# Summing four of a pair's seven products in one PSUM bank, with ScalarE copies between the groups

## The chip, the cores and the metric

One core of one Trainium2 chip runs the whole program. The metric is the device time of one execution in microseconds (us). TensorE (PE) multiplies matrices into PSUM, an accumulator memory of eight banks; VectorE (DVE) and ScalarE (ACT) read PSUM and work in SBUF; GpSimd (POOL) and SyncE (SP) mostly issue DMAs here. Each engine works through its own queue in order and waits on semaphores of the others.

## The reference

Two layers of a decoder trunk over 544 token columns (512 of a prompt, 32 of eight short samples). What matters is the large matrix products: two SwiGLU feed-forward blocks of each layer, and the input projection of the mixers with its sigmoid gates.

```
h = rmsnorm(x, g);  gate, up = split(h @ w_up)          # 1024 -> 2 x 2816
x = x + 0.5 * (silu(gate) * up) @ w_down                # 2816 -> 1024, twice in a layer
z = rmsnorm(x, g_mix) @ w_in                            # 1024 -> 6144
u = gelu(z[u]);  g = sigmoid(z[gates])                  # the parts of z that the change touches
merged = g0 * y_a + g1 * y_b + g2 * y_c;  x = x + merged @ w_o
```

## The kernel before

**Tiling.** Activations lie transposed in SBUF: 128 partitions by 544 tokens, and `HT` = 272 is half of them. Every product is made of three matmuls, since operands are split into a high and a low part: low weight by high input, high by high, high by low. Weights stream from memory as *units* of 512 columns. `unit` first stages later units: it issues loads (SP, for some units with an accumulating POOL DMA, L223 to L231), adds two raw blocks on VectorE (L237, `split_add`), takes the high part on ScalarE (L244, `split_hi`) and the low part on VectorE (L249, `split_lo`), four to six units ahead of the one in use. The order on every engine is the order in which the code is written; a tile framework adds the semaphores.

**Pairs.** Two blocks of 128 outputs by 544 tokens make a *pair*. `s_pair` computes it with seven products of half size in place of eight, in Winograd's form: the weights and the token halves are summed and subtracted beforehand (`s_inputs`, `split_add`), seven products named W21, R3, W22, R1, R2, R4 and W12 are made (`PRODUCTS`), and their results are combined into the four quarters of the pair. Each product is 12 matmuls of 128x272 (`mm_s`, L325), one unit of weights. A pair's halves are called h1 and h2; its two result tiles are `a` (s1) and `b` (s2). One ScalarE copy (L579) and seven VectorE operations (L581, L583, L587, L588, L589, L591, L593) read the products from PSUM. There are 109 pairs. 81 are in the feed-forward blocks (`ff_group`): there `d0` (L620) multiplies the gate tile by `rstd`, and later steps, spread over the following units by `tick`, apply Silu (`dz`), multiply by `rstd` (`dr`), multiply gate and up (`d1`) and split the result (`d2`, `d3`). The other 28 are in the mixers: a sigmoid (L858) or a gelu (L956) follows over both tiles.

**PSUM.** Four tiles `ps0` to `ps3` hold two banks each. `ring_bank` hands out one bank at a time (tile n%4, its other half after a turn); `bank`, used by `gemm` for the down projections (L302, added to x at L660) and other plain products, hands out whole tiles from the same counter. A pair takes seven ring banks. Between pairs stand plain products (a down projection behind 52 of the feed-forward pairs, another product behind the 28 of the mixers) or, behind 29 pairs, the next pair.

Of the kernel before, what the change touches and what calls it, by code (L numbers as in the profile page):

```python
# [63 lines left out]

Z_U, Z_V, Z_B, Z_C, Z_XB, Z_XC, Z_G = 0, 4, 8, 12, 16, 20, 24

PRODUCTS = (("W21", "B11"), ("R3", "T2"), ("W22", "B21"), ("R1", "T1"), ("R2", "T3"), ("R4", "B22"), ("W12", "T4"))
N_WEIGHTS = L * (2 * (D * 2 * DFF + DFF * D) + D * 48 * P + 3 * SEQ * D + G * P * P + 2 * D * D + NPLE * P * D)


# [32 lines left out]
class Kern:  # L103
# [214 lines left out]
                hooks[n]()  # L318
        return pst

    def mm_s(self, ps, w, xs, q, first, last):
        wh, wl = (a[:, q * P:(q + 1) * P] for a in w)
        xh, xl = xs
        for i, (a, b) in enumerate(((wl, xh), (wh, xh), (wh, xl))):
            self.nc.tensor.matmul(ps, a, b, start=first and i == 0, stop=last and i == 2)  # L325

    def s_unit(self, i, name, l, m1, m2):
        assert self.left == 0
# [74 lines left out]
    def s_inputs(self, gain, full):  # L403
        nc = self.nc
        h1, h2 = slice(0, HT), slice(HT, T)
        inp = Inputs(gain)
        sets, tiles, sl, zs = inp.sets, inp.tiles, inp.sl, inp.zs

        def steps(q):
            st = {}  # L410
            sets.append({})

            def load():
                st["e"] = [self.slot() for _ in range(2)]
# [12 lines left out]
            def hi_b():  # L427
                E1, E2 = (e[0] for e in st["e"]) if full else (self.x[2 * q], self.x[2 * q + 1])
                g1, g2 = (1.0, 1.0) if full else (gain(2 * q), gain(2 * q + 1))
                a, b = own(*self.rpair()), own(*self.rpair())  # L430
                if full:
                    st["b"] = [(E1[:, :], a[0][:, :], a[1][:, :], g1)]
                    tiles.append((a[0][:, :], a[1][:, :]))
                else:
                    z = self.slot(F32R)
                    zs.append(z)
                    z = z[0]
                    st["b"] = [(E1[:, h1], a[0][:, h1], a[1][:, h1], g1), (E1[:, h2], z[:, h1], z[:, h2], g1)]
                    tiles.append(((a[0][:, h1], z[:, h1]), (a[1][:, h1], z[:, h2])))
                st["b"].append((E2[:, :], b[0][:, :], b[1][:, :], g2))  # L440
                tiles.append((b[0][:, :], b[1][:, :]))
                for src, hi, lo, g in st["b"]:
                    nc.scalar.activation(hi, src, AF.Copy, scale=g)  # L443
                st["a"] = a
                for n, t, h in (("B11", a, h1), ("B21", b, h1), ("B22", b, h2)):
                    sets[q][n] = (t[0][:, h], t[1][:, h])

            def lo_b():
                for src, hi, lo, g in st["b"]:
                    if full:  # L450
                        nc.vector.tensor_sub(lo, src, hi.bitcast(F32))
                    else:
                        nc.vector.scalar_tensor_tensor(lo, src, g, hi.bitcast(F32), op0=ALU.mult, op1=ALU.subtract)

            def sums():
                A, E = (e[0] for e in st["e"])
                st["t"] = self.slot()
                B = st["t"][0]
                nc.vector.tensor_sub(A[:, h1], A[:, h1], A[:, h2])
                nc.vector.tensor_sub(B[:, h2], A[:, h2], E[:, h2])  # L460
                nc.vector.tensor_add(B[:, h1], E[:, h2], A[:, h1])
                nc.vector.tensor_sub(A[:, h2], E[:, h1], B[:, h1])
# [101 lines left out]
        self.psi += 1  # L564
        return self.ps[n % 4][:, n // 4 % 2, :]

    def s_pair(self, name, l, m1, m2, sets, s1, s2):
        nc = self.nc
        h1, h2 = slice(0, HT), slice(HT, T)
        q_ = self.slot()  # L570
        q1, V = q_[0][:, h1], q_[0][:, h2]
        a, b = s1[0], s2[0]
        for i, (w, x) in enumerate(PRODUCTS):
            bk = self.ring_bank()[:, :HT]
            wt = self.s_unit(i, name, l, m1, m2)
            for q, xs in enumerate(sets):
                self.mm_s(bk, wt, xs[x], q, q == 0, q == len(sets) - 1)
            if w == "W21":
                nc.scalar.activation(q1, bk, AF.Copy)  # L579
            elif w == "R3":  # L580
                nc.vector.tensor_sub(V, bk, q1)  # L581
            elif w == "W22":
                nc.vector.tensor_add(b[:, h1], bk, q1)  # L583
            elif w == "R1":
                b5 = bk
            elif w == "R2":
                nc.vector.tensor_add(a[:, h1], bk, V)  # L587
                nc.vector.tensor_sub(V, V, b5)  # L588
                nc.vector.tensor_sub(a[:, h2], a[:, h1], b5)  # L589
            elif w == "R4":  # L590
                nc.vector.tensor_sub(b[:, h2], bk, V)  # L591
            else:
                nc.vector.tensor_add(a[:, h1], a[:, h1], bk)  # L593
            self.tick()
        self.drop(q_)

    def ff_group(self, up, l, j, inp, first, plain, hs, hsl):
        nc = self.nc
# [44 lines left out]
            else:  # L643
                fin = (e0, dz, e1, dr, d2, d3)
        else:
            self.s_pair(up, l, NFF + j, j, inp.sets, o_, t_)
            d0()
            fin = (dz, dr, d1, d2, d3)
        self.later += [(1 + i, f) for i, f in enumerate(fin) if f]

# [71 lines left out]
    def mix(self, l, inp, nxt):  # L722
# [11 lines left out]
        def W2(z):  # L734
            return ("w_in", l, z, xr, 0)

        def pair(z1, z2):
# [115 lines left out]

        def branch(br, ys, wn, mid=None):
            for m in range(0, KD, 2):
                ts = pair(Z_G + br * KD + m, Z_G + br * KD + m + 1)
                for t_ in ts:
                    nc.scalar.activation(t_[0][:, :], t_[0][:, :], AF.Sigmoid)  # L858
                if m == 0 and mid:
                    mid()  # L860
                for i, t_ in enumerate(ts):
                    t = t_[0]
                    py, = self.gemm([(wn, l, m + i, ys, 0)])
                    nc.vector.tensor_mul(self.v2(t[:, :]), self.pv(py), self.v2(t[:, :]))  # L864
                    if len(macc) < KD:
                        macc.append(t_)
                        continue
                    mc = macc[m + i][0]
                    nc.vector.tensor_add(mc[:, :], mc[:, :], t[:, :])
                    self.drop(t_)  # L870
                    if br == 0 and self.used < USE_MERGE and len(merged) == m + i:
                        merge(m + i)
# [79 lines left out]
        us = []  # L952

        def u_in(j):
            for t_ in pair(Z_U + j, Z_U + j + 1):
                nc.scalar.activation(t_[0][:, :], t_[0][:, :], AF.Gelu_apprx_tanh)  # L956
                us.append(t_)

        def c_mid():
            c_mix()  # L960
# [311 lines left out]
```

## Time and profile before

| | us |
|---|---|
| median of 3 runs | 2436.96 (2435.14 to 2437.22) |
| span of the profiled execution | 2435.3 |
| TensorE busy | 2414.3 (99%) |
| VectorE busy | 1903.0 (78%) |
| ScalarE busy | 1087.3 (45%) |

The profile shows the execution by its span alone; the median lies 1.7 us above it. A row of a group reads: line, engine, operation, output and inputs, shapes, count, busy us and mean ns of one, then the idle time before it and what ended that. TensorE's ends are modelled, and a matmul's duration is longer than the distance to the next one, since they are pipelined.

### The profile page before, as it was taken

The numbers are of one execution on the slowest core, as the hardware profiler recorded it, in microseconds if no ns is written. First come the engines' busy times: TensorE is split into PE (matmuls) and PEld (weight loads), VectorE is DVE, ScalarE is ACT, GpSimd is POOL, SyncE is SP. The second block draws the span as 40 slices with busy tenths as digits, with TensorE's granted clock in tenths as the row PEclk, the third lists the DMA queues.
The fourth block names the chain that finished last, engine by engine and source line by source line (L and its number), as shares of the span: only waits on it lengthen the run. The fifth ranks groups of instructions, "written<-read, shape, count | busy, mean of one in ns | idle before, by whom it ended". The sixth has DMA issues, their size and how long they took to land.

```text
span 2435.3 us, 48371 instructions
## 1 busy us (share of the span) xinstructions
PE 2414.3 (99%) x19016; PEld 2401.5 (99%) x19016; DVE 1903.0 (78%) x3583; ACT 1087.3 (45%) x2021; POOL 202.0 (8%) x248
## 2 busy tenths in 40 slices
PE   8999999999999999999999999999999999999997
PEld 8999999999999999999999999999999999999997
DVE  7887776778788887878788777866788779877775
ACT  6443444444446444435554444434354454434352
POOL 1111000010110100100010110000011011101000
PEclk9999999999999999999999999999999999999998
DMA  6665551354554555555255565523455536656521
GB/s 199 143 148 140 148 163 58 88 143 118 145 158 114 141 144 145 148 139 157 63 139 142 135 157 137 161 70 82 128 133 146 165 91 145 157 131 154 145 80 38
DMA packets 173988, 318.79 MB, mean 131 GB/s; under 512 B 19584, under 2 KB 21888, under 8 KB 173760
## 3 DMA queue, kind: packets, MB, share of 16 engines
q1 hardware_dynamic: 139248, 252.24, 34.2%
q0 software_dynamic: 32640, 61.16, 15.0%
q8 instruction: 149, 2.44, 0.4%
q10 hardware_dynamic: 1872, 2.29, 0.3%
q14 instruction: 79, 0.65, 0.1%
HBM read 312.63 MB, written 2.99 MB: 130 GB/s over the span
## 4 chain that ended last, share of the span: by engine, by line
PE 99%; DVE 0%; ACT 0%; DMA 0%; issue 0%; DVEq 0%; ACTq 0%
PE ps L325 47%; PE ps L302 46%; PE ps L807 2%; PE ps L1069 2%; PE ps L530 0%; PE ps L516 0%; PE ps L972 0%; DMA par<-in_par 0%; DVE s L1114 0%; PE ps L974 0%; DVE x L1096 0%; ACT s L1100 0%; ACT L502 0%; ACT L244 0%; DVE s L1095 0%
## 5 line engine op out<-in xcount | busy, mean ns | idle before, releaser
L325 PE MATMUL ps<-s,s 128*128 128x272 f32 x9156 | 1162.0, 288 | 0.0
L325 PEld LDWEIGHTS ps<-s,s 128*128 128x128 f32 x9156 | 1153.5, 188 | 0.4 <-DVE s L938 0.2
L302 PE MATMUL ps<-s,s 128*128 128x272 f32 x8880 | 1132.6, 288 | 7.3 <-ACT s L443 7.3
L302 PEld LDWEIGHTS ps<-s,s 128*128 128x128 f32 x8880 | 1121.7, 189 | 7.6 <-ACT s L443 7.2
L244 ACT ACTIVATE s<-s 128x512 fp32r<-128x512 f32 x1169 | 663.1, 621 | 506.0 <-DVE s L237 461.6
L249 DVE TENSOR_TENSOR s<-s,s 128x512 fp32r<-128x512 f32 x1169 | 768.3, 685 | 8.6 <-ACT s L244 8.6
L231 POOL DMA_DIRECT2D s<-in_wts x218 | 186.0, 854 | 1738.2 <-DMA s<-in_wts 448.5
L660 DVE SCALAR_TENSOR_TENSOR x<-ps,x 128x544 f32<-128x544 f32 x128 | 92.4, 722 | 137.2 <-PE ps L302 137.0
L579 ACT ACTIVATE s<-ps 128x272 f32<-128x272 f32 x109 | 43.2, 396 | 251.3 <-PE ps L325 251.1
L237 DVE TENSOR_TENSOR s<-s,s 128x512 f32<-128x512 f32 x218 | 149.3, 685 | 0.0
L581 DVE TENSOR_TENSOR s<-ps,s 128x272 f32<-128x272 f32 x109 | 48.0, 441 | 69.5 <-PE ps L325 43.3
L587 DVE TENSOR_TENSOR s<-ps,s 128x272 f32<-128x272 f32 x109 | 48.1, 441 | 63.8 <-PE ps L325 62.7
L607 ACT ACTIVATE s<-s 128x544 f32<-128x544 f32 x88 | 57.9, 658 | 89.4 <-DVE s L620 89.0
L613 ACT ACTIVATE s<-s 128x544 fp32r<-128x544 f32 x88 | 57.6, 654 | 59.8 <-DVE s L610 44.1
L864 DVE TENSOR_TENSOR s<-ps,s 128x544 f32<-128x544 f32 x48 | 34.8, 725 | 50.7 <-PE ps L302 46.2
L616 DVE TENSOR_TENSOR s<-s,s 128x544 fp32r<-128x544 f32 x88 | 63.2, 718 | 5.9 <-ACT s L613 5.8
L1069 PE MATMUL ps<-s,s 128*128 128x256 f32 (+1 forms) x480 | 61.6, 289 | 1.8 <-ACT rstd L532 1.8
L623 DVE TENSOR_TENSOR s<-s,rstd 128x544 f32<-128x544 f32 x88 | 63.2, 718 | 0.1
L1069 PEld LDWEIGHTS ps<-s,s 128*128 128x128 f32 x480 | 60.5, 188 | 2.0 <-ACT rstd L532 2.0
L610 DVE TENSOR_TENSOR s<-s,s 128x544 f32<-128x544 f32 x82 | 58.9, 718 | 0.4
L858 ACT ACTIVATE s<-s 128x544 f32<-128x544 f32 x48 | 29.0, 652 | 67.6 <-DVE s L593 67.6
L620 DVE TENSOR_TENSOR s<-s,rstd 128x544 f32<-128x544 f32 x82 | 59.0, 719 | 0.0
(133 smaller groups left out, 1176.4 us busy)
## 6 DMA issues: line engine op xcount, KB each, us to landing
s<-in_wts SPq DMA_DIRECT2D x951, 256.0 KB, 3.4
s<-in_wts POOLq DMA_DIRECT2D x218, 256.0 KB, 4.6
x<-in_xT ACTq DMA_DIRECT2D x4, 272.0 KB, 5.2
x<-in_xT SPq DMA_DIRECT2D x4, 272.0 KB, 4.8
s<-in_pT POOLq DMA_DIRECT2D x4, 272.0 KB, 3.2
out_yT<-s SPq DMA_DIRECT2D x4, 144.0 KB, 1.8
out_yT<-s ACTq DMA_DIRECT2D x4, 144.0 KB, 1.8
s<-in_st_in POOLq DMA_DIRECT2D x2, 272.0 KB, 3.1
```

Source lines behind the costliest of these rows:

```text
L231: self.nc.gpsimd.dma_start(out=t, in_=src(1 if w == "R1" else 2, 4), accum_op=ALU.add)
L237: self.nc.vector.tensor_add(self.new_raw(w, u0, 2 if w == "R3" else 1), self.read_raw(a, u0), self.read_raw(b, u0))
L244: self.nc.scalar.activation(a[0][:, :UC], self.read_raw(w, u0), AF.Copy)
L249: self.nc.vector.tensor_sub(lo, self.read_raw(w, u0), hi.bitcast(F32))
L302: self.nc.tensor.matmul(ps[:, h, :HT], a, bh, start=first and i == 0, stop=last and i == 2)
L325: self.nc.tensor.matmul(ps, a, b, start=first and i == 0, stop=last and i == 2)
L610: nc.vector.tensor_mul(o[:, :], o[:, :], t[:, :])
L616: nc.vector.tensor_sub(lo, o[:, :], hi.bitcast(F32))
L620: nc.vector.tensor_mul(t[:, :], t[:, :], self.rstd[:, :])
L623: nc.vector.tensor_mul(o[:, :], o[:, :], self.rstd[:, :])
L660: nc.vector.scalar_tensor_tensor(xm, self.pv(pst[i]), 0.5, xm, op0=ALU.mult, op1=ALU.add)
L1069: nc.tensor.matmul(ps, a, b[:, c], start=first and i == 0, stop=last and i == 2)
```

## The change

- `PRODUCTS` is put in another order: W21, R2, R3, W22, R1, W12, R4.
- A pair takes four ring banks, X, Y, Z and V. W21, R3, R1 and R4 are summed in X, each group going on from the last with no start flag. R2 goes to Y, W22 to Z, W12 to V.
- Between the groups in X, ScalarE copies the running sum out: after W21, after R3 and after R1 (L580, L582 and L587 of the changed kernel).
- VectorE has four operations for a pair (L583, L585, L588, L590). `sums` (signs of the input sums) is adapted, with the same number of operations.
- The last sum, after R4, is read by a function `last`: in feed-forward pairs VectorE multiplies X by `rstd` (L649), and the other half of the tile is multiplied by itself (L650) in place of `d0`. In the mixers ScalarE applies the sigmoid or gelu on X (L742), then on the rest (L744, L745).

```diff
     def s_pair(self, name, l, m1, m2, sets, s1, s2, last=None):
-        q_ = self.slot()
-        q1, V = q_[0][:, h1], q_[0][:, h2]
         a, b = s1[0], s2[0]
+        X, Y, Z, V = (self.ring_bank()[:, :HT] for _ in range(4))
+        bank = {"W21": X, "R2": Y, "R3": X, "W22": Z, "R1": X, "W12": V, "R4": X}
         for i, (w, x) in enumerate(PRODUCTS):
-            bk = self.ring_bank()[:, :HT]
+            bk = bank[w]
             wt = self.s_unit(i, name, l, m1, m2)
+            new = w in ("W21", "R2", "W22", "W12")
             for q, xs in enumerate(sets):
-                self.mm_s(bk, wt, xs[x], q, q == 0, q == len(sets) - 1)
+                self.mm_s(bk, wt, xs[x], q, new and q == 0, q == len(sets) - 1, not new)
             if w == "W21":
-                nc.scalar.activation(q1, bk, AF.Copy)
+                nc.scalar.activation(b[:, h1], X, AF.Copy)
             elif w == "R3":
-                nc.vector.tensor_sub(V, bk, q1)
+                nc.scalar.activation(a[:, h2], X, AF.Copy)
+                nc.vector.tensor_sub(a[:, h1], Y, a[:, h2])
             elif w == "W22":
-                nc.vector.tensor_add(b[:, h1], bk, q1)
+                nc.vector.tensor_add(b[:, h1], Z, b[:, h1])
             elif w == "R1":
-                b5 = bk
-            elif w == "R2":
-                nc.vector.tensor_add(a[:, h1], bk, V)
-                nc.vector.tensor_sub(V, V, b5)
-                nc.vector.tensor_sub(a[:, h2], a[:, h1], b5)
+                nc.scalar.activation(b[:, h2], X, AF.Copy)
+                nc.vector.tensor_sub(a[:, h2], Y, b[:, h2])
+            elif w == "W12":
+                nc.vector.tensor_add(a[:, h1], V, a[:, h1])
             elif w == "R4":
-                nc.vector.tensor_sub(b[:, h2], bk, V)
-            else:
-                nc.vector.tensor_add(a[:, h1], a[:, h1], bk)
+                if last:
+                    last(b[:, h2], X)
+                else:
+                    nc.scalar.activation(b[:, h2], X, AF.Copy)
...
-            self.s_pair(up, l, NFF + j, j, inp.sets, o_, t_)
-            d0()
+            r = self.rstd
+            self.s_pair(up, l, NFF + j, j, inp.sets, o_, t_,
+                        lambda out, ps: nc.vector.tensor_mul(out, ps, r[:, HT:]))
+            nc.vector.tensor_mul(t[:, :HT], t[:, :HT], r[:, :HT])
...
+        def pair(z1, z2, f=None):
             s1, s2 = self.slot(), self.slot()
-            self.s_pair("w_in", l, z1, z2, sets, s1, s2)
+            self.s_pair("w_in", l, z1, z2, sets, s1, s2, (lambda out, ps: nc.scalar.activation(out, ps, f)) if f else None)
+            if f:
+                nc.scalar.activation(s2[0][:, :HT], s2[0][:, :HT], f)
+                nc.scalar.activation(s1[0][:, :], s1[0][:, :], f)
```

TensorE at the end of the first pair, whose next work is a down projection (L302). The tiles `ps_71` to `ps_74` are `ps0` to `ps3`. Before:

```order
L325 MATMUL ps_74<-s_117_618,s_149_862 128x272
L325 MATMUL ps_74<-s_117_618,s_148_861 128x272 x2
L325 MATMUL ps_74<-s_131_699,s_149_862 128x272
L325 MATMUL ps_74<-s_131_699,s_148_861 128x272 x2
L302 MATMUL ps_71<-s_35_167,s_152_881 128x272 [waits DVE_49]
```

In the changed kernel:

```order
L325 MATMUL ps_72<-s_23_141,s_147_860 128x272
L325 MATMUL ps_72<-s_24_142,s_147_860 128x272
L325 MATMUL ps_72<-s_30_156,s_148_861 128x272
L325 MATMUL ps_72<-s_30_156,s_147_860 128x272
L325 MATMUL ps_72<-s_31_157,s_147_860 128x272
L302 MATMUL ps_72<-s_35_167,s_151_879 128x272 [waits DVE_49]
```

The pair's last product and the down projection stood in different tiles before; now both stand in the tile that holds X, with a wait on VectorE between them.

VectorE at the end of a feed-forward pair that a down projection follows (`ps_74` holds X in the changed kernel). Before:

```order
L589 TENSOR_TENSOR s_549_3456<-s_549_3456,ps_72 128x272
L249 TENSOR_TENSOR s_565_3538<-s_531_3299,s_564_3537 128x512 [waits DMAHW2_49,Activation_49]
L237 TENSOR_TENSOR s_569_3561<-s_538_3342,s_535_3323 128x512 [waits DMAHW3_49,DMASW4_49]
L591 TENSOR_TENSOR s_548_3455<-ps_74,s_552_3459 128x272 [waits DVE_49,PE_49]
L249 TENSOR_TENSOR s_568_3559<-s_535_3323,s_567_3558 128x512 [waits Activation_49]
L593 TENSOR_TENSOR s_549_3456<-s_549_3456,ps_71 128x272 [waits DVE_49,PE_49]
L620 TENSOR_TENSOR s_548_3455<-s_548_3455,rstd 128x544 [waits DVE_49]
```

In the changed kernel:

```order
L588 TENSOR_TENSOR s_535_3441<-ps_71,s_534_3440 128x272 [waits DVE_49,Activation_49]
L249 TENSOR_TENSOR s_551_3525<-s_518_3287,s_550_3524 128x512 [waits DMAHW2_49]
L590 TENSOR_TENSOR s_535_3441<-ps_73,s_535_3441 128x272 [waits PE_49]
L249 TENSOR_TENSOR s_554_3546<-s_521_3308,s_553_3545 128x512 [waits DMAHW3_49,Activation_49]
L237 TENSOR_TENSOR s_558_3567<-s_528_3350,s_521_3308 128x512 [waits DMASW5_49]
L649 TENSOR_TENSOR s_534_3440<-ps_74,rstd 128x272 [waits DVE_49,PE_49]
L650 TENSOR_TENSOR s_534_3440<-s_534_3440,rstd 128x272
```

The last read of PSUM, L593 before, is now L649, which reads X itself; one (49 pairs) or two (32 pairs, as here) staging operations stand between it and the fourth combining operation, L590.

ScalarE in a pair of the mixers at which the activation table changes. Before:

```order
L244 ACTIVATE s_1159_7495<-s_1157_7474 128x512 [waits DVE_49,PE_49]
L244 ACTIVATE s_1162_7514<-s_1119_7282 128x512 [waits DMAHW4_49,PE_49]
L956 ACT_TABLE_LOAD
L956 ACTIVATE s_1140_7392<-s_1140_7392 128x544 [waits DVE_49]
L956 ACTIVATE s_1141_7393<-s_1141_7393 128x544 [waits Activation_49]
```

In the changed kernel:

```order
L587 ACTIVATE s_1118_7370<-ps_72 128x272 [waits PE_49]
L244 ACTIVATE s_1134_7469<-s_1092_7238 128x512 [waits DMASW6_49,DVE_49]
L244 ACTIVATE s_1138_7491<-s_1136_7472 128x512 [waits DVE_49]
L742 ACT_TABLE_LOAD [waits PE_49]
L742 ACTIVATE s_1118_7370<-ps_72 128x272 [waits Activation_49]
L744 ACTIVATE s_1118_7370<-s_1118_7370 128x272
```

The table load, which stood free ahead of an operation on SBUF, now stands between the wait for TensorE and the read of X; it does so in 8 of the 10 pairs of the mixers that have one.

## Rows read from the trace of the kernel before

**Rows 1.** The page's part on engines: busy us, share of the span, instructions.
```profile
PE 2414.3 (99%) x19016; PEld 2401.5 (99%) x19016; DVE 1903.0 (78%) x3583; ACT 1087.3 (45%) x2021; POOL 202.0 (8%) x248
```
**Rows 2.** The page's chain that ended last, as shares of the span by engine.
```profile
PE 99%; DVE 0%; ACT 0%; DMA 0%; issue 0%; DVEq 0%; ACTq 0%
```
**Rows 3.** Waits of PE: who waited for whom, us in total, times, longest.
```profile
PE ps L302 <- ACT s L443: 7.3, 1, 7.3
...
PE ps L1069 <- ACT rstd L532: 1.8, 1, 1.8
```
**Rows 4.** The chain in order of time: start us, us, what; two unbroken stretches.
```profile
2001.38 42.13 PE ps L325 x336
...
2318.91 36.10 PE ps L302 x288
```
**Rows 5.** Groups by line: count, busy us, mean ns, idle before.
```profile
L325 PE MATMUL ps<-s,s 128*128 128x272 f32 x9156 | 1162.0, 288 | 0.0
...
L620 DVE TENSOR_TENSOR s<-s,rstd 128x544 f32<-128x544 f32 x82 | 59.0, 719 | 0.0
...
L587 DVE TENSOR_TENSOR s<-ps,s 128x272 f32<-128x272 f32 x109 | 48.1, 441 | 63.8 <-PE ps L325 62.7
...
L579 ACT ACTIVATE s<-ps 128x272 f32<-128x272 f32 x109 | 43.2, 396 | 251.3 <-PE ps L325 251.1
...
L858 ACT ACTIVATE s<-s 128x544 f32<-128x544 f32 x48 | 29.0, 652 | 67.6 <-DVE s L593 67.6
...
L858 ACT ACT_TABLE_LOAD x6 | 7.7, 1283 | 0.1
...
L956 ACT ACTIVATE s<-s 128x544 f32<-128x544 f32 x8 | 4.8, 650 | 7.2 <-DVE s L593 7.2
```
**Rows 6.** Timeline of TensorE from the start of a pair: start us, us, what.
```profile
605.22 1.93 PE L325 MATMUL ps<-s,s 128*128 128x272 f32 x14
```
**Rows 7.** Timeline of ScalarE and VectorE in the same pair.
```profile
606.93 0.40 ACT L579 ACTIVATE s<-ps 128x272 f32<-128x272 f32 x1 [0.81 <-PE ps L325]
...
612.96 0.44 DVE L587 TENSOR_TENSOR s<-ps,s 128x272 f32<-128x272 f32 x1 [0.76 <-PE ps L325]
...
613.79 0.43 DVE L589 TENSOR_TENSOR s<-s,ps 128x272 f32<-128x272 f32 x1
614.14 0.68 DVE L249 TENSOR_TENSOR s<-s,s 128x512 fp32r<-128x512 f32 x1
614.74 0.43 DVE L591 TENSOR_TENSOR s<-ps,s 128x272 f32<-128x272 f32 x1
```
**Rows 8.** Timeline near the end, where PE waits for a bank that ACT reads.
```profile
2400.53 1.04 PE L1069 MATMUL ps<-s,s 128*128 128x288 f32 x6
...
2402.91 0.37 ACT L532 ACTIVATE rstd<-ps 128x256 f32<-128x256 f32 x1
...
2403.33 0.93 PE L1069 MATMUL ps<-s,s 128*128 128x288 f32 x5 [1.76 <-ACT rstd L532]
```
**Rows 9.** The same place, a narrower window of TensorE alone.
```profile
2403.33 0.53 PE L1069 MATMUL ps<-s,s 128*128 128x288 f32 x2 [1.76 <-ACT rstd L532]
```
**Rows 10.** Waits of ACT: us in total, times, longest us.
```profile
ACT s L244 <- DVE s L237: 461.6, 180, 5.4
```
**Rows 11.** Windows near the end: length, busy us (count) of PE, PEld, DVE, ACT, POOL; granted clock; DMA.
```profile
2400.00:2403.00 3.00, 1.57 (x13) 1.33 (x11) 2.39 (x6) 2.17 (x4) 0.00 (x0) 1.00 0.00 0
2424.00:2428.00 4.00, 2.18 (x10) 2.09 (x10) 1.64 (x9) 0.37 (x2) 0.00 (x0) 0.50 0.00 0
```

More of the change, by code (lines that the diff above doesn't have):

```diff
@@ L65 @@
 Z_U, Z_V, Z_B, Z_C, Z_XB, Z_XC, Z_G = 0, 4, 8, 12, 16, 20, 24
-PRODUCTS = (("W21", "B11"), ("R3", "T2"), ("W22", "B21"), ("R1", "T1"), ("R2", "T3"), ("R4", "B22"), ("W12", "T4"))
+PRODUCTS = (("W21", "B11"), ("R2", "T3"), ("R3", "T2"), ("W22", "B21"), ("R1", "T1"), ("W12", "T4"), ("R4", "B22"))
 N_WEIGHTS = L * (2 * (D * 2 * DFF + DFF * D) + D * 48 * P + 3 * SEQ * D + G * P * P + 2 * D * D + NPLE * P * D)
@@ L319, in gemm, with mm_s @@
         return pst
-    def mm_s(self, ps, w, xs, q, first, last):
+    def mm_s(self, ps, w, xs, q, first, last, go_on=False):
         wh, wl = (a[:, q * P:(q + 1) * P] for a in w)
@@ L324, in mm_s @@
         for i, (a, b) in enumerate(((wl, xh), (wh, xh), (wh, xl))):
-            self.nc.tensor.matmul(ps, a, b, start=first and i == 0, stop=last and i == 2)
+            self.nc.tensor.matmul(ps, a, b, start=first and i == 0, stop=last and i == 2, skip_group_check=go_on)
     def s_unit(self, i, name, l, m1, m2):
@@ L458, in sums @@
                 B = st["t"][0]
+                nc.vector.tensor_sub(B[:, h2], A[:, h2], E[:, h2])
+                nc.vector.tensor_sub(B[:, h1], B[:, h2], A[:, h1])
                 nc.vector.tensor_sub(A[:, h1], A[:, h1], A[:, h2])
-                nc.vector.tensor_sub(B[:, h2], A[:, h2], E[:, h2])
-                nc.vector.tensor_add(B[:, h1], E[:, h2], A[:, h1])
-                nc.vector.tensor_sub(A[:, h2], E[:, h1], B[:, h1])
+                nc.vector.tensor_add(A[:, h2], E[:, h1], B[:, h1])
                 self.drop(st["e"][1])
@@ L565, in ring_bank, with s_pair @@
         return self.ps[n % 4][:, n // 4 % 2, :]
-    def s_pair(self, name, l, m1, m2, sets, s1, s2):
+    def s_pair(self, name, l, m1, m2, sets, s1, s2, last=None):
         nc = self.nc
         h1, h2 = slice(0, HT), slice(HT, T)
-        q_ = self.slot()
-        q1, V = q_[0][:, h1], q_[0][:, h2]
         a, b = s1[0], s2[0]
+        X, Y, Z, V = (self.ring_bank()[:, :HT] for _ in range(4))
+        bank = {"W21": X, "R2": Y, "R3": X, "W22": Z, "R1": X, "W12": V, "R4": X}
         for i, (w, x) in enumerate(PRODUCTS):
-            bk = self.ring_bank()[:, :HT]
+            bk = bank[w]
             wt = self.s_unit(i, name, l, m1, m2)
+            new = w in ("W21", "R2", "W22", "W12")
             for q, xs in enumerate(sets):
-                self.mm_s(bk, wt, xs[x], q, q == 0, q == len(sets) - 1)
+                self.mm_s(bk, wt, xs[x], q, new and q == 0, q == len(sets) - 1, not new)
             if w == "W21":
-                nc.scalar.activation(q1, bk, AF.Copy)
+                nc.scalar.activation(b[:, h1], X, AF.Copy)
             elif w == "R3":
-                nc.vector.tensor_sub(V, bk, q1)
+                nc.scalar.activation(a[:, h2], X, AF.Copy)
+                nc.vector.tensor_sub(a[:, h1], Y, a[:, h2])
             elif w == "W22":
-                nc.vector.tensor_add(b[:, h1], bk, q1)
+                nc.vector.tensor_add(b[:, h1], Z, b[:, h1])
             elif w == "R1":
-                b5 = bk
-            elif w == "R2":
-                nc.vector.tensor_add(a[:, h1], bk, V)
-                nc.vector.tensor_sub(V, V, b5)
-                nc.vector.tensor_sub(a[:, h2], a[:, h1], b5)
+                nc.scalar.activation(b[:, h2], X, AF.Copy)
+                nc.vector.tensor_sub(a[:, h2], Y, b[:, h2])
+            elif w == "W12":
+                nc.vector.tensor_add(a[:, h1], V, a[:, h1])
             elif w == "R4":
-                nc.vector.tensor_sub(b[:, h2], bk, V)
-            else:
-                nc.vector.tensor_add(a[:, h1], a[:, h1], bk)
+                if last:
+                    last(b[:, h2], X)
+                else:
+                    nc.scalar.activation(b[:, h2], X, AF.Copy)
             self.tick()
-        self.drop(q_)
     def ff_group(self, up, l, j, inp, first, plain, hs, hsl):
@@ L855, in branch @@
             for m in range(0, KD, 2):
-                ts = pair(Z_G + br * KD + m, Z_G + br * KD + m + 1)
-                for t_ in ts:
-                    nc.scalar.activation(t_[0][:, :], t_[0][:, :], AF.Sigmoid)
+                ts = pair(Z_G + br * KD + m, Z_G + br * KD + m + 1, AF.Sigmoid)
                 if m == 0 and mid:
@@ L954, in u_in @@
         def u_in(j):
-            for t_ in pair(Z_U + j, Z_U + j + 1):
-                nc.scalar.activation(t_[0][:, :], t_[0][:, :], AF.Gelu_apprx_tanh)
-                us.append(t_)
+            us.extend(pair(Z_U + j, Z_U + j + 1, AF.Gelu_apprx_tanh))
         def c_mid():
```

1 line of the change is left out of this document (removed).

## The prediction

> **What bounds the kernel now.** I read the page's engine part first: TensorE is busy for 2414.3 of 2435.3 us, VectorE for 78%, ScalarE for 45% [rows 1]. The chain that ended last says the same in another way: 99% of it is TensorE [rows 2]. So I looked for TensorE's waits. There are four in the whole execution, at the start and at the end; the longest is 7.3 us, the last 1.8 us [rows 3]. Between them TensorE never waits for anybody, neither in a pair nor behind one. Then its pace: a stretch of four pairs has 336 matmuls in 42.13 us, and a stretch of plain products 288 in 36.10 us [rows 4]. Both are 125.4 ns for a matmul, 1.505 us for a product of twelve and 10.53 us for a pair. One matmul alone lasts 288 ns by its row [rows 5], since they overlap.
>
> From this follow two things. Work taken from VectorE or ScalarE is worth nothing by itself: it lies beside an engine that waits for neither. And each wait that TensorE meets in the middle is paid in full, since nothing later has slack to give it back.
>
> **The change part by part.** *VectorE's operations.* Three of seven go, 109 times, at some 0.44 us (the row of L587 [rows 5]): 144 us of VectorE's time. In the 81 feed-forward pairs two half multiplications of 0.44 us take the place of one of 0.72 us (L620) [rows 5], which gives 13 us back. (28 of the 109 pairs are in the mixers: 48 and 8 sigmoids and gelus, two for a pair [rows 5].) ScalarE gets two more copies of 0.396 us (L579 [rows 5]) for each pair, 86 us, and in the mixers a readout in two pieces. All of this is hidden by TensorE: gain and cost nothing.
>
> *The number of matmuls, units and loads* stays. Products in another order move each load and split with its product, at the same lead of four units and more. Nothing.
>
> *The waits inside a pair.* R3, R1 and R4 now go on in the bank that ScalarE copies, so each waits for the copy. Between W21 and R3 lies R2, between R3 and R1 lies W22, between R1 and R4 lies W12: each time one product, 1.505 us, for the copy to be made. A pair's first matmul stands at 605.22 [rows 6]; the twelfth starts 11 x 0.1254 us later and ends 0.288 us after that, at 606.89, and the copy starts at 606.93 [rows 7], 0.04 us later. It takes 0.396 us. So the bank is free 0.44 us after the product's end and is wanted 1.1 us later still. The cover is W22, R2 or W12, and it is enough unless ScalarE comes over 1 us late. I take nothing.
>
> *The wait behind a pair.* Here there is no product in between. R4 is the last, and its sum is read by L649 on VectorE or L742 on ScalarE. TensorE's next work stands in the same tile: a down projection or another plain product takes the whole tile, and a pair that follows takes its other bank, but waits all the same, as the order shows for all 109 pairs. Before, the last tile read was not the next one written. What one such wait costs:
> - TensorE's pipeline runs dry: 0.288 less the usual 0.125 is 0.16 us [rows 4, 5].
> - From its end to the reader's start: 0.04 us for ScalarE as above. For VectorE, L587 waits for the 60th matmul, which starts at 605.22 + 59 x 0.1254 = 612.62 and ends at 612.91; it starts at 612.96 [rows 7], so 0.05 us.
> - The readout of 128x272: 0.441 us on VectorE, 0.396 us on ScalarE [rows 5].
> - From its end to TensorE: near the end TensorE waits for a bank that ScalarE reads. ScalarE ends at 2402.91 + 0.37 and TensorE goes on at 2403.33 [rows 8]: 0.05 us.
> - The restart: there the first two matmuls take 0.53 us together, so the second starts 0.24 us after the first [rows 9]; five take 0.93 us [rows 8], so the later distances are 0.13. That is 0.11 us more than usual.
>
> Sum: 0.81 us behind a feed-forward pair, 0.76 us in the mixers. 81 x 0.814 = 65.9 us and 28 x 0.759 = 21.3 us.
>
> Is the reader there in time? L649 stands behind L590, which must wait for the end of W12, and behind one or two staging operations. Half operations follow each other at 0.35 us, a split at 0.60 us (613.79, 614.14, 614.74) [rows 7]. With two it takes 0.35 + 2 x 0.60 = 1.55 us against R4's 1.505 us: late by some 0.05 us, in 32 pairs, 2 us in all. With one, in 49 pairs, it is there 0.5 us early. In the mixers ScalarE has only splits ahead of L742. But in 8 pairs the table load stands behind the wait for TensorE, so its 1.283 us [rows 5] come on top: 10.3 us.
>
> Together 65.9 + 21.3 + 1.8 + 10.3 = 99 us on the profiled span of 2435.3 us. The median of the runs lies 1.7 us above it, and the sum is put on the median: 2436.96 + 99 = 2536 us, 4.1% slower.
>
> Bounds. The smallest price of a wait: the reader frees the bank at its back-to-back distance of 0.35 us [rows 7] and the restart is free, 0.16 + 0.05 + 0.35 + 0.05 = 0.61 us, and the table loads hide. That is 109 x 0.61 = 66 us, 2503 us. A gain is excluded there, since TensorE can't write a tile before R4's sum has been read. The largest is the first rival's. I stay with the middle, whose rows show this very kind of wait.
>
> **The rivals.**
> *Late readers.* VectorE is loaded to four fifths now, and ScalarE often waits for VectorE's sums before a split: 461.6 us, 180 times, at worst 5.4 us [rows 10]. Copies of X stand behind such splits, and VectorE's subtractions now wait for ScalarE's copies, which wasn't so before. If each feed-forward readout comes one more split late (0.60 us), that is 81 x 0.60 = 49 us more: 2585 us. The point from which it decides is 1.5 us of VectorE's work behind W12's end. For it: the 32 pairs are at that point already. Against: VectorE loses 130 us of work.
>
> *The clock falls.* If TensorE's granted clock fell to 1.2 GHz for the product behind each wait, its twelve matmuls would take twice 125 ns: 1.5 us, 109 times, 164 us more, 2700 us. Near the end TensorE is idle for 1.43 us of three and keeps a granted clock of 1.00 (2.4 GHz); only after longer idling is it 0.50 [rows 11]. My waits idle it for 0.6 us in 10 to 17. So little speaks for it. The Trainium skill's page "TensorE: Matmul & The Clock Gate", section "A second HAM failure mode: psum-queue depth-cycling", tells of a kernel whose short idle times between groups in cycled PSUM banks made the clock oscillate; by that rule this rival would come true, and the trace does not bear it out.
>
> *Not slower.* If a matmul's 125.4 ns were held up by VectorE's reads of PSUM, fewer of them would quicken all 18036 matmuls of that shape; from 99 us / 18036 = 5.5 ns each it would pay the waits back, 2437 us or less. Against it stands that the pace is the same in pairs, with eight readouts of seven products, as in plain products [rows 4]. The same page, section "HAM oscillation — how this bites in real kernels", reports that double-buffering PSUM gave one kernel no further gain; by that a wait on a bank would cost nothing and the time would stay at 2437. The one wait of this kind in the trace was not free [rows 8].
>
> **How the numbers follow.** The forecast, 2536 us with 2515 to 2565 around it, gets 70%. Late readers 12%, the cheap wait (near 2503) 8%, the clock 4%, not slower 6%. The range 2503 to 2590 holds the forecast, most of the late readers and of the cheap wait, and leaves out the clock and the last case. A measurement of this kernel can tell 0.2% (5 us) from no change; slower than that 0.94, within it 0.04, faster 0.02.
>
> **What would show it.** TensorE's waits should list 81 for L649 and 28 for L742, some 0.54 and 0.49 us each as rows show idle time (the dry pipeline is hidden in the modelled ends), with the loads some 68 us, and TensorE at 97% of the span. A pair still takes 10.5 us from its first matmul to its last. Waits inside pairs, for L580, L582 and L587, should be absent. VectorE should fall by some 130 us and ScalarE rise by some 90. The forecast is wrong if TensorE waits elsewhere, if the clock is below 1 in the middle, or if the distance between matmuls changes.

## The result and the profile after

The changed kernel takes 2567.97 us (median of 4 runs, 2567.88 to 2568.18), the kernel before 2436.32 us in the same comparison. The ratio is 1.0539, with an interval of 1.0525 to 1.0553. It is slower by 131.6 us, where the prediction said 99 us (2536 us, 2503 to 2590). The profiled span is 2566.5 us, 131.2 us more than before.

The page of the changed kernel, engines and then the chain that ended last; they answer to [rows 1] and [rows 2].

```profile
PE 2455.6 (96%) x19016; PEld 2417.1 (94%) x19016; DVE 1808.5 (70%) x3337; ACT 1167.1 (45%) x2267; POOL 201.9 (8%) x248
...
PE 86%; DVE 8%; ACT 4%; issue 2%; DMA 0%; DVEq 0%; SPq 0%; ACTq 0%
```

VectorE has 94 us less to do and the kernel is slower: the chain that was TensorE's at 99% now runs through VectorE and ScalarE for 12% of the span. TensorE's waits say where (who waited for whom, us in total, times, longest); they answer to [rows 3].

```profile
PE ps L302 <- DVE s L649: 41.4, 52, 1.1
PE ps L302 <- ACT s L742: 24.9, 26, 2.3
PE ps L325 <- DVE s L649: 16.7, 29, 0.7
PE ps L302 <- ACT s L443: 6.9, 1, 6.9
PE ps L325 <- ACT s L580: 5.9, 9, 1.2
...
PE ps L974 <- ACT s L742: 1.2, 2, 0.6
```

The waits for L649 are 52 + 29 = 81, those for L742 are 26 + 2 = 28: one behind each pair. In the 29 of L325 the next pair writes the other bank of X's tile, so there TensorE waits for the tile as a whole and not for a bank that it needs. New as well are the waits for L580, the copy of W21, inside pairs.

A pair whose reader is on time, with the next pair behind it: timeline of VectorE and TensorE.

```profile
105.69 0.44 DVE L649 TENSOR_TENSOR s<-ps,rstd 128x272 f32<-128x272 f32 x1 [0.35 <-PE ps L325]
106.05 0.43 DVE L650 TENSOR_TENSOR s<-s,rstd 128x272 f32<-128x272 f32 x1
106.19 1.94 PEld L325 LDWEIGHTS ps<-s,s 128*128 128x128 f32 x15 [0.76 <-DVE s L649]
106.19 2.03 PE L325 MATMUL ps<-s,s 128*128 128x272 f32 x14 [0.53 <-DVE s L649]
```

VectorE stands ready 0.35 us before the sum is, reads for 0.44 us, and TensorE goes on 0.06 us later, after 0.53 us of idle time. The weight load starts in the same moment as the matmul: it waits too, and isn't made ahead.

**Where the 131 us sit.** Idle rows hide a part, since matmul ends are modelled. So I took the distance from each matmul's start to the next and subtracted the usual 0.1254 us:

| | us | predicted |
|---|---|---|
| 81 waits behind feed-forward pairs, reader on time (0.801 each) | 64.9 | 65.9 |
| 28 waits behind pairs of the mixers, reader on time (0.755 each) | 21.1 | 21.3 |
| late readers behind feed-forward pairs | 14.9 | 1.8 |
| late readers in the mixers (8 table loads above all) | 12.5 | 10.3 |
| waits inside pairs for the copy of W21 (10 pairs) | 8.6 | 0 |
| six stretches at half clock | 9.0 | 0 |
| sum | 131.0 | 99.3 |

The price of a wait on time is the median from the run `readout_first` below, in which no reader is late; in the changed kernel itself the late part is what its waits take above that. The six stretches are those in the middle of the execution, counted as time lost.

**A late reader.** VectorE in a pair that a down projection follows, and TensorE behind it:

```profile
161.06 0.44 DVE L588 TENSOR_TENSOR s<-ps,s 128x272 f32<-128x272 f32 x1 [0.38 <-ACT s L587]
161.41 0.72 DVE L617 TENSOR_TENSOR s<-s,s 128x544 fp32r<-128x544 f32 x1
162.04 0.68 DVE L249 TENSOR_TENSOR s<-s,s 128x512 fp32r<-128x512 f32 x1
162.65 0.43 DVE L590 TENSOR_TENSOR s<-ps,s 128x272 f32<-128x272 f32 x1
163.00 0.68 DVE L249 TENSOR_TENSOR s<-s,s 128x512 fp32r<-128x512 f32 x1
163.60 0.69 DVE L237 TENSOR_TENSOR s<-s,s 128x512 f32<-128x512 f32 x1
164.20 0.43 DVE L649 TENSOR_TENSOR s<-ps,rstd 128x272 f32<-128x272 f32 x1
...
164.69 2.52 PE L302 MATMUL ps<-s,s 128*128 128x272 f32 x18 [1.10 <-DVE s L649]
```

From 161.06 on VectorE has no idle time. L588 waited for ScalarE's copy L587, then an older step (L617, `d3` of an earlier pair) and a split come ahead of L590, and two staging operations ahead of L649. R4's sum was there at 163.6; it is read 0.6 us later. 23 of the 81 waits have a lag of over 0.5 us, six more one of 0.2 us, and these 29 are just the pairs in which L617 stands between L588 and L590. Of the other 52, 16 are late by some 0.05 us (two staging operations ahead of L649), and 36 are on time.

**A late copy inside a pair**, ScalarE and TensorE at the start of a block:

```profile
842.31 0.66 ACT L614 ACTIVATE s<-s 128x544 fp32r<-128x544 f32 x1 [1.55 <-DVE s L624]
842.87 0.38 ACT L580 ACTIVATE s<-ps 128x272 f32<-128x272 f32 x1
...
843.30 2.90 PE L325 MATMUL ps<-s,s 128*128 128x272 f32 x21 [0.65 <-ACT s L580]
```

W21 was done some 1.5 us earlier, but ScalarE works in order, and ahead of the copy stood an operation that waited 1.55 us for VectorE. R3 comes 1.5 us behind W21, and the copy wasn't made. Of the ten such waits three stand at the start of a feed-forward block, as here, one in the first block, and six in the mixers.

**A table load behind the wait**, ScalarE in the mixers, and the windows behind this wait and behind an ordinary one (length, busy us and count of PE, PEld, DVE, ACT, POOL; granted clock; DMA):

```profile
642.85 1.28 ACT L742 ACT_TABLE_LOAD   x1 [0.31 <-PE ps L325]
644.14 0.40 ACT L742 ACTIVATE s<-ps 128x272 f32<-128x272 f32 x1
...
645.60:649.40 3.80, 3.80 (x21) 3.80 (x20) 0.00 (x1) 1.36 (x3) 0.00 (x0) 0.55 0.10 17
663.50:669.70 6.20, 6.20 (x50) 6.20 (x51) 2.15 (x4) 2.34 (x5) 0.00 (x0) 1.00 0.39 90
```

ScalarE waited for R4's sum and only then loaded the table for 1.28 us; the sum was read 1.29 us late. Behind that wait TensorE's granted clock is 0.55 for 3.8 us, that is, at 1.2 GHz for most of it; 21 matmuls stand where 30 fit. Behind an ordinary wait it is 1.00.

### The profile page after: what moved, and what is told of

Read it like the earlier page. It is cut to its first block, busy times and chain, and to the rows that moved or that the text cites. A ratio compares the mean times of both kernels' runs of the same rounds, so it can differ in the third digit from the quotient of the medians.

```text
span 2566.5 us, 48078 instructions
## 1 busy us (share of the span) xinstructions
PE 2455.6 (96%) x19016; PEld 2417.1 (94%) x19016; DVE 1808.5 (70%) x3337; ACT 1167.1 (45%) x2267; POOL 201.9 (8%) x248
## 4 chain that ended last, share of the span: by engine, by line
PE 86%; DVE 8%; ACT 4%; issue 2%; DMA 0%; DVEq 0%; SPq 0%; ACTq 0%
PE ps L302 43%; PE ps L325 37%; PE ps L1071 2%; PE ps L813 2%; DVE s L249 2%; DVE s L649 1%; DVE s L237 1%; DVE s L588 1%; DVE s L617 1%; ACT s L587 1%; DVE s L590 1%; ACT s L244 1%; ACT s L742 0%; PE ps L530 0%; DMA s<-in_wts 0%
## 5 line engine op out<-in xcount | busy, mean ns | idle before, releaser
L302 PE MATMUL ps<-s,s 128*128 128x272 f32 x8880 | 1148.9, 291 | 73.1 <-DVE s L649 41.4
L302 PEld LDWEIGHTS ps<-s,s 128*128 128x128 f32 x8880 | 1128.7, 190 | 90.3 <-DVE s L649 52.8
L325 PE MATMUL ps<-s,s 128*128 128x272 f32 x9156 | 1172.5, 289 | 22.6 <-DVE s L649 16.7
L325 PEld LDWEIGHTS ps<-s,s 128*128 128x128 f32 x9156 | 1155.9, 188 | 31.3 <-DVE s L649 23.0
L249 DVE TENSOR_TENSOR s<-s,s 128x512 fp32r<-128x512 f32 x1169 | 780.9, 685 | 34.7 <-ACT s L244 33.4
L244 ACT ACTIVATE s<-s 128x512 fp32r<-128x512 f32 x1169 | 673.2, 621 | 204.8 <-DVE s L237 202.2
L580 ACT ACTIVATE s<-ps 128x272 f32<-128x272 f32 x109 | 43.2, 397 | 562.9 <-PE ps L325 562.9
L663 DVE SCALAR_TENSOR_TENSOR x<-ps,x 128x544 f32<-128x544 f32 x128 | 92.7, 724 | 240.5 <-PE ps L302 240.2
L583 DVE TENSOR_TENSOR s<-ps,s 128x272 f32<-128x272 f32 x109 | 48.1, 442 | 113.9 <-ACT s L582 113.4
L868 DVE TENSOR_TENSOR s<-ps,s 128x544 f32<-128x544 f32 x48 | 34.8, 725 | 115.2 <-PE ps L302 115.2
L582 ACT ACTIVATE s<-ps 128x272 f32<-128x272 f32 x109 | 43.3, 397 | 99.3 <-PE ps L325 99.3
L588 DVE TENSOR_TENSOR s<-ps,s 128x272 f32<-128x272 f32 x109 | 48.1, 442 | 56.4 <-ACT s L587 55.9
L587 ACT ACTIVATE s<-ps 128x272 f32<-128x272 f32 x109 | 43.1, 396 | 97.5 <-PE ps L325 97.5
L617 DVE TENSOR_TENSOR s<-s,s 128x544 fp32r<-128x544 f32 x88 | 63.4, 721 | 6.1 <-ACT s L614 5.8
L608 ACT ACTIVATE s<-s 128x544 f32<-128x544 f32 x88 | 57.8, 657 | 19.9 <-DVE s L650 18.1
L624 DVE TENSOR_TENSOR s<-s,rstd 128x544 f32<-128x544 f32 x88 | 63.4, 721 | 0.1
```

The source lines that it names most:

```text
L244: self.nc.scalar.activation(a[0][:, :UC], self.read_raw(w, u0), AF.Copy)
L249: self.nc.vector.tensor_sub(lo, self.read_raw(w, u0), hi.bitcast(F32))
L302: self.nc.tensor.matmul(ps[:, h, :HT], a, bh, start=first and i == 0, stop=last and i == 2)
L587: nc.scalar.activation(b[:, h2], X, AF.Copy)
L588: nc.vector.tensor_sub(a[:, h2], Y, b[:, h2])
L617: nc.vector.tensor_sub(lo, o[:, :], hi.bitcast(F32))
```

## The experiments

My theory after the result: TensorE pays nothing but waits on PSUM tiles that a reader hasn't left yet, and each in full. The rivals: that the change itself costs (copies, sums that go on, other VectorE work), that the waits are cheap and something else is dear, that the clock pays most of it, or that fewer reads of PSUM by VectorE are worth something. All runs are timed against the kernel before (2436.9 us, 7 runs, for before_same_tile, other_tile, readout_first and table_early; 2437.3 us, 15 runs, for x_first_skip, w21_own and readout_triple).

### The kernel before, with its next work in the tile read last (before_same_tile)

```diff
             self.tick()
         self.drop(q_)
+        self.psi += 3
```

> The kernel before with one line added at the end of a pair that moves the ring on by three, so that the next work stands in the tile of the pair's last product; VectorE keeps its seven operations and ScalarE its one copy. Theory (the tile alone makes the loss): each of 109 pairs is followed by a wait for L593 of some 0.8 us, and more where VectorE comes late, as the trace of before shows it coming 0.2 to 0.4 us late at L593: 87 to 130 us more, 2523 to 2570 us. Rival (the new way of summing makes the loss): within 10 us of before, 2437 us.

Measured: 2568.02 us (2565.56 to 2569.21), ratio 1.0537 (1.0521 to 1.0552): 131 us slower, as much as the changed kernel. TensorE's waits:

```profile
PE ps L302 <- DVE s L593: 70.4, 78, 1.8
PE ps L325 <- DVE s L593: 28.5, 29, 1.5
```

One moved counter, with all seven VectorE operations in place, costs what the whole change costs. The theory held. That the sums agree to 0.1 us is chance: here the distances have 118.4 us of waits, 11.4 of restarts and one stretch at half clock (1.5 us), the readers are late more often, and there are no waits inside pairs.

### X in the last of the four banks (other_tile)

```diff
-        X, Y, Z, V = (self.ring_bank()[:, :HT] for _ in range(4))
+        Y, Z, V, X, _ = (self.ring_bank()[:, :HT] for _ in range(5))
```

> The changed kernel with X in the fourth of a pair's ring banks instead of the first, and one ring bank left out behind it, so that TensorE's next work never stands in X's tile; nothing else is altered. Theory (the loss is TensorE's wait for the readout of X behind each pair, with the clock falling only after the longest of these waits): TensorE's waits for L649 and L742 vanish, the clock stays at 1.00 in the middle, only the some 8 us of waits for the W21 copy (L580) remain: 2440 to 2450 us. Rival (the copies on ScalarE, the summing in one bank or the late VectorE cost by themselves): still over 2500 us.

Measured: 2529.43 us (2528.63 to 2530.33), ratio 1.038 (1.0364 to 1.0395). The expectation was missed by 80 us, and the time is where the rival put it (over 2500 us). TensorE's waits, and the timeline at one:

```profile
PE ps L325 <- DVE x L663: 39.2, 48, 0.8
PE ps L325 <- DVE s L868: 16.3, 20, 0.8
...
141.85 0.72 DVE L663 SCALAR_TENSOR_TENSOR x<-ps,x 128x544 f32<-128x544 f32 x1 [2.28 <-PE ps L302]
...
142.62 2.65 PE L325 MATMUL ps<-s,s 128*128 128x272 f32 x19 [0.81 <-DVE x L663]
```

Nothing waits for L649 or L742 any more: behind the pairs the distances have 0.0 us. But 78.6 us stand ahead of them now, with 8.0 us of restarts, 3.4 us for copies of W21 and 1.2 us of slow clock: together 91 of the 92 us. There are four tiles; the fourth one from the counter is the tile that was handed out just before the pair, and L663, the add of the down projection, still reads it when W21 wants it. (L868 does the same in the mixers.) I had looked at who waits behind X and not at who stood in its tile before. The wait wasn't removed, it was moved from a pair's end to its start: evidence for the theory of waits, against my reading of the ring. The time alone would not tell this from the rival; the next run does.

### X first, one bank skipped (x_first_skip)

```diff
-        X, Y, Z, V = (self.ring_bank()[:, :HT] for _ in range(4))
+        X, Y, Z, V, _ = (self.ring_bank()[:, :HT] for _ in range(5))
```

> The changed kernel with X still the first of its four ring banks, but the next ring bank left unused, so that the work behind a pair starts in Y's tile (read for the last time behind R1, two products earlier), and X stays clear of the tile that the work ahead of the pair wrote last. If the whole loss is waits on tiles that their reader hasn't left: both the wait behind a pair and the one that a last tile had at the pair's start are gone; what stays are the some ten waits of R3 for the copy of W21, 8.6 us, since the slow stretches of the clock followed only the long waits: 2437 + 9 = 2446 us, 2441 to 2452. If the change in itself costs more (the copies, the restarts, sums in a bank that goes on with no start flag): over 2465. If the three VectorE operations that went are worth something to TensorE: under 2437.

Measured: 2446.18 us (2443.75 to 2446.47), ratio 1.0033 (1.0022 to 1.0045): 8.9 us slower than before. TensorE's waits in the middle and the page's engines:

```profile
PE ps L325 <- ACT s L580: 5.7, 7, 1.2
...
PE 2417.5 (99%) x19016; PEld 2403.0 (98%) x19016; DVE 1805.0 (74%) x3337; ACT 1166.9 (48%) x2267; POOL 201.5 (8%) x248
```

The waits behind pairs are gone, those ahead too, and with them the slow clock in the middle. What is left, 8.7 us by the distances, are the ten waits for the copy of W21 (seven of them show as idle time). So 122 of the 131 us were the choice of a bank and what hung on it; three copies, sums that go on without a start flag and the new order of products cost TensorE nothing else. Nor did the VectorE operations that went give anything back. The Trainium skill's page "Perfetto Trace Analysis", section "Matmuls", advises to rotate independent matmul groups through different PSUM banks, so that the emptying of one lies beside the next group's matmuls. The two runs agree with it, 2529 against 2446 us, and add that the tile has to be clear on both sides of the work, the one ahead and the one behind.

### W21 in a bank of its own (w21_own)

```diff
-        X, Y, Z, V = (self.ring_bank()[:, :HT] for _ in range(4))
-        bank = {"W21": X, "R2": Y, "R3": X, "W22": Z, "R1": X, "W12": V, "R4": X}
+        Q, Y, X, Z, V = (self.ring_bank()[:, :HT] for _ in range(5))
+        bank = {"W21": Q, "R2": Y, "R3": X, "W22": Z, "R1": X, "W12": V, "R4": X}
...
-            new = w in ("W21", "R2", "W22", "W12")
+            new = w in ("W21", "R2", "R3", "W22", "W12")
...
-                nc.scalar.activation(b[:, h1], X, AF.Copy)
+                nc.scalar.activation(b[:, h1], Q, AF.Copy)
```

> W21 gets a bank of its own (Q; ring order Q, Y, X, Z, V), R3 starts a new sum, and W21 is left out of the later sums of X, so a part of the result is missing; the number of matmuls, copies and VectorE operations is that of the changed kernel. R3 waits for no copy now, and the work behind a pair starts in Y's tile. If the 8.6 us of waits inside pairs are all that is left beside the wait behind a pair: 2437 us, 2434 to 2441. If a late copy behind W21 only passes its lateness on to the copy behind R3: 2442 to 2446, with waits for L582. Nothing here can be under 2434 unless fewer VectorE readouts quicken the matmuls.

Measured: 2440.65 us (2439.88 to 2441.25), ratio 1.0014 (1.0005 to 1.0024): 3.4 us slower than before. The waits for L580 are gone; in their place:

```profile
PE ps L325 <- ACT s L582: 2.4, 4, 0.9
...
579.88 1.15 ACT L244 ACTIVATE s<-s 128x512 fp32r<-128x512 f32 x2 [1.24 <-DVE s L237]
580.94 0.38 ACT L582 ACTIVATE s<-ps 128x272 f32<-128x272 f32 x1
...
581.37 1.89 PE L325 MATMUL ps<-s,s 128*128 128x272 f32 x13 [0.85 <-ACT s L582]
```

The time lies inside my first range, at its upper end, but the mechanism is partly the second: in four of the ten pairs the copy behind R3 is now late, by 3.5 us in all. In the one shown ScalarE is behind because of its own queue: two splits stand ahead of the copy, and the first of them waited 1.24 us for VectorE. All four lie in the mixers. So 5 of the 8.6 us were W21's bank, and the rest is ScalarE's lateness there.

### The readout ahead of the staging (readout_first)

```diff
-    def unit(self, entry):
+    def unit(self, entry, late=False):
...
+        self.late = lambda: self.ahead(entry)
+        if not late:
+            self.ahead(entry)
...
-            wt = self.s_unit(i, name, l, m1, m2)
+            wt = self.s_unit(i, name, l, m1, m2, w == "R4")
...
                     nc.scalar.activation(b[:, h2], X, AF.Copy)
+                self.late()
```

`ahead` holds the staging of later units, which `unit` did at once. For R4 it is put off, and `self.late()` does it after the readout.

> The changed kernel with the staging of later units that stood between R4's matmuls and the readout of X put behind the readout. Theory (some 22 feed-forward readouts come 0.6 us late because one split and one sum stand ahead of L649 on VectorE, some others 0.05 us): the wait behind those pairs falls from 1.38 to 0.82 us, some 13 us in all: 2552 to 2557 us. Rival (the lateness comes from further up, from L588 or L590): the waits stay as they are and the time within 4 us of 2568 us, or a new wait for staged weights takes the gain back.

Measured: 2530.5 us (2530.41 to 2532.81), ratio 1.0387 (1.037 to 1.0404). The gain on the changed kernel is 37 us, not 13, and the time lies 22 us under the expected range. TensorE's waits, then ScalarE's groups for the readout in the mixers (count, busy us, mean ns, idle before):

```profile
PE ps L308 <- DVE s L656: 27.7, 52, 0.5
PE ps L331 <- DVE s L656: 15.5, 29, 0.5
PE ps L308 <- ACT s L749: 12.7, 26, 0.5
...
L749 ACT ACT_TABLE_LOAD x10 | 12.8, 1283 | 1.0 <-DVE s L594 0.7
...
L749 ACT ACTIVATE s<-ps 128x272 f32<-128x272 f32 x28 | 11.1, 397 | 44.0 <-PE ps L331 41.8 <-DVE s L249 2.1
```

(Lines lie 6 or 7 further down here: L656 is L649, L749 is L742.) The longest wait is 0.5 us, so no reader is late. The waits for VectorE fall from 58.1 to 43.2 us; that is the part that I expected. I had not expected the mixers: 24.9 to 12.7 us. With the readout in front, it has to wait for VectorE and TensorE; in the changed kernel it was TensorE, with the load behind that wait, and ScalarE itself. The order on ScalarE now shows the table load carrying the wait for VectorE and the activation the one for TensorE:

```
L749 ACT_TABLE_LOAD [waits DVE_49]
L749 ACTIVATE s_1118_7370<-ps_72 128x272 [waits PE_49]
```

So the load is done while R4 runs. And with the long waits the half clock went, 9.0 us. 14.9 + 12.2 + 9.0 = 36.1 us.

This run also gives the clean price of a wait: a median of 0.801 us for a feed-forward pair and 0.755 us in the mixers, restart and all.

### The table loaded early (table_early)

```diff
+                if warm:
+                    warm()
...
+                        (lambda: nc.scalar.activation(self.cols[:, 39:40], self.ones[:, 0:1], f)) if f else None)
```

Behind W12 a sigmoid or gelu of one column is run in the mixers, so the table is there before R4 ends.

> The changed kernel with a sigmoid or gelu of one column, 128x1, put behind W12 of each pair of the mixers, so that a table load happens before ScalarE waits for R4. Theory (8 readouts carry a table load of 1.3 us, and the six short spells of half clock follow just these long waits): 8 x 1.33 us and all six spells go, together some 20 us: 2546 to 2551 us. Rival (the clock falls from the share of idle time, not from the long waits): the spells stay, some 11 us: 2556 to 2559 us.

Measured: 2548.0 us (2547.21 to 2550.01), ratio 1.0457 (1.0441 to 1.0473): 20 us less than the changed kernel.

```profile
PE ps L302 <- ACT s L744: 14.7, 26, 0.8
```

The waits in the mixers fall by 10.2 us, and not one stretch of low clock is left in the middle, another 9.0 us. The theory held: in the changed kernel the slow clock followed from the long waits that the table loads made.

### The readout three times over (readout_triple)

```diff
-                        lambda out, ps: nc.vector.tensor_mul(out, ps, r[:, HT:]))
+                        lambda out, ps: [nc.vector.tensor_mul(out, ps, r[:, HT:]) for _ in range(3)])
```

> The changed kernel, with the feed-forward readout of X done three times over (the same product written again). If each wait behind a pair is paid in full: two more operations at a distance of 0.35 to 0.44 us each in 81 pairs, 57 to 71 us on 2568: 2625 to 2639 us, and the waits of TensorE for VectorE grow from 58 to some 115 to 129 us. If TensorE's clock also falls behind waits of this length (1.5 to 2.2 us; so far it fell only behind waits of 2.1 to 2.6 us), each such spell adds some 1.5 us: 2640 to 2760. If part of it is hidden by slack further on: under 2615.

Measured: 2665.18 us (2662.65 to 2667.58), ratio 1.0938 (1.092 to 1.0957): 97 us more than the changed kernel. Timeline of the readout in the pair shown above, TensorE's waits, and windows behind one of the long ones:

```profile
106.72 1.39 DVE L649 TENSOR_TENSOR s<-ps,rstd 128x272 f32<-128x272 f32 x3 [0.36 <-PE ps L325]
...
PE ps L302 <- DVE s L649: 90.8, 52, 2.1
PE ps L325 <- DVE s L649: 44.2, 29, 1.7
...
170.60:171.60 1.00, 1.00 (x4) 1.00 (x5) 1.00 (x3) 0.74 (x2) 0.00 (x0) 0.50 0.16 61
171.60:175.00 3.40, 3.40 (x21) 3.40 (x21) 2.31 (x4) 1.48 (x3) 0.00 (x0) 0.67 0.00 0
175.00:177.00 2.00, 2.00 (x19) 2.00 (x18) 0.18 (x1) 0.00 (x0) 0.00 (x0) 1.00 0.34 116
```

Three readouts take 1.39 us, so each added one costs 0.475 us, not 0.35 to 0.44: they write the same half of a tile, and the next starts 0.03 us after the last has ended. The waits for VectorE grow to 135.0 us for that reason, above the 115 to 129 that I expected. 81 x 2 x 0.475 = 77.0 us; the distances behind pairs grew by exactly that, from 101.7 to 178.7 us. Each wait is paid in full. Of the other 20 us, 19 are the clock: 27.7 us lost at half clock, 9.0 in the changed kernel. So both parts of the expectation came true, the second within its range (2640 to 2760).

## Why the prediction was right, and where it fell short

**The number.** The mechanism is the one forecast, a wait of TensorE behind each pair, and the time lies inside 2503 to 2590 us. It lies 3 us above the band 2515 to 2565 that got 70%, and the loss is 131.6 us against 99. Some 18 of the missing 32 us are terms that the sum put at nothing (waits inside pairs, the clock), 15 are late readers. The range reached so far only because of a rival that came true by a third (15 of its 49 us), and that left room for terms it was not made for: in this the range was lucky. Two of the three signs of being wrong that the prediction named did come: TensorE waits for L580 inside pairs, and the clock is below 1 in the middle. The third, another distance between matmuls, did not.

**What bounds the kernel.** Right. TensorE had no slack, so every wait was paid: in readout_triple 77.0 us of added readouts made the waits 77.0 us longer, and none of it was given back.

**Operations taken from VectorE are worth nothing.** Right: with the bank out of the way the kernel was not faster than before. The size was off: 94 us of busy time went, not 130. I had multiplied by the duration of 0.44 us, but in a row of operations each fills only its distance to the next, 0.35 us (the durations added up fell by 127 us). ScalarE rose by 80 us, not 90. Neither has any effect on the time.

**The price of a wait behind a pair.** Right, and the best of the steps: 0.81 and 0.76 us were put together from rows of five places, 0.801 and 0.755 us were measured with every reader on time. The parts hold too: in the pair on time above, 0.03 us to the reader, 0.44 us of reading and 0.06 us back. As idle time 0.54 and 0.49 us were expected; in readout_first they are 43.2 / 81 = 0.53 and 12.7 / 26 = 0.49. All waits behind pairs were to be 68 us; with the late readers they are 84. The restart of 0.11 us measured 0.10. The number of waits, 81 and 28, is as forecast.

**Is the reader there in time?** This step failed: 1.8 us taken, 14.9 us measured. I took it that L590 is done right behind W12 and counted only the staging between it and L649. In the late pairs VectorE was already behind: L588 waits for a ScalarE copy, and where the older step L617 stands behind it, L590 comes 0.55 to 1.2 us behind W12's end. The 0.05 us taken for 32 pairs was right for the 16 of them without L617. The rival "late readers" named that chain, with a price of 49 us; 23 of 81 pairs were late by the 0.6 us that it assumed for all.

**The table loads.** 10.3 us predicted. Eight loads by the lag that was measured, and four small lags, make 12.5.

**The waits inside a pair.** This step failed too: taken as nothing, 8.6 us measured. The slack of 1.1 us was enough in 99 pairs; in ten, at starts of blocks and in the mixers, ScalarE was later than that, in the one shown because what stands ahead of the copy waits for VectorE. "Unless ScalarE comes over 1 us late" was written, and not looked up; [rows 10] had 5.4 us as its longest wait.

**The clock.** The rival was set aside for the wrong reason, in part. It was priced for waits of 0.6 us, and behind those the clock indeed stayed at 1.00. But the forecast itself had eight waits with a table load in them, over 2 us long, and behind six of these eight the clock fell: 9.0 us. The row it rested on, a granted clock of 1.00 near the end [rows 11], was one execution's: behind the same wait there (2.07 us by the distance) the clock fell to 0.50 in six of the nine profiles of this case, that of the changed kernel among them. The Trainium skill's page "TensorE: Matmul & The Clock Gate", section "A second HAM failure mode: psum-queue depth-cycling", has the clock oscillate with frequent short idle times between groups. This case does not bear that out: behind the 101 shorter of the 109 waits the clock stayed at 1.00.

**Not slower, and the cheap wait.** Both fell. The run with three readouts shows that no part of a wait is given back. The Trainium skill's page "TensorE: Matmul & The Clock Gate", section "HAM oscillation — how this bites in real kernels", reports that double-buffering PSUM gave one kernel no further gain. In this kernel it is otherwise: a tile that is clear on both sides is worth 122 us.

**What stays open.** The table comes within 0.2 us of the difference of the spans. It leaves out a seventh stretch at half clock in the changed kernel, near its end, which costs some 1.7 us by the distances and isn't in the profile of before; the distances between the other matmuls add up to 1.2 us less than before. Why the clock fell behind some of the waits of over 2 us and not behind others, the runs don't tell. No version faster than the kernel before was found, and none is to be expected along this line as long as TensorE is the bound, with 19016 matmuls in both.

## What to carry to other kernels

When TensorE is the bound, cost a change by the first instruction of each group that it makes wait, and ask of every accumulator both who read its tile last ahead of it and who writes it next. An accumulator that has to be emptied with no other work between cost 0.8 us here each time, so let the group that is read last stand in a tile that nobody wants for another product's time. Work taken from an engine with slack is worth nothing, but work that is put in the path between two engines (a copy, a staging operation, a table load ahead of the readout) is paid in full.

## What the runs showed of the hardware

- **The weight load waits too.** At 106.19 the load and the matmul start together, and the first distances behind a wait are longer by 0.10 us in all.
- **A table load stands among the waits.** In 8 of the 10 pairs of the mixers that have one, the wait for TensorE stands ahead of the load (0.31 us idle, then 1.28 us of load, with R4's sum ready). In the other two, and in all ten of readout_first, the wait ahead of the load is that for VectorE, the activation carries the one for TensorE, and the load was hidden. In the kernel before, where the sigmoid or gelu waits for VectorE alone, all ten loads stand free ahead of that wait.
- **Readouts that write the same half of a tile follow each other at 0.475 us; onto another half it is 0.36 us**: 1.39 us for three, against 105.69 and 106.05 in the rows above.
- **TensorE's clock behind a wait.** By the distance from the last matmul ahead of a wait to the first behind it, and in the middle of the executions, the granted clock fell to 0.50 (1.2 GHz) behind 27 of 42 waits of 2.1 to 2.6 us (6 of 8 in the changed kernel, 19 of 31 with three readouts, 1 of 1 in before_same_tile, 1 of 2 in other_tile), each time for some 3.4 us. It fell behind none of the 83 waits of 1.5 to 2.0 us (58 with three readouts, 25 in before_same_tile), and behind none of the shorter ones.
